# Nine instead of seven up-projection pairs in seven products each, placed two and two, in a one-core encoder layer

## The chip, the core and the metric

The kernel runs on one core of one Trainium2 chip. The metric is the time of one execution in microseconds (us), as the device reports it; three runs of the kernel before are shown, and one further execution was profiled. A lower time is better.

## What is computed

One layer of an encoder with 512 tokens and a model width of 1024, all in float32. Three sub-layers follow one another, each between two RMS norms and added to the residual: token mixing (an attention group and a gated recurrent group, "HGRN"), cross-attention into 256 memory tokens, and a gated MLP. The change is mostly about the MLP:

```python
def conv_ffn(h, w_up, conv_w, conv_b, w_down):
    u = h @ w_up                       # 512 x 1024 times 1024 x 5632
    up = jnp.pad(u, ((0, 0), (half, half), (0, 0)))
    acc = conv_b
    for j in range(CONV_W):
        acc = acc + up[:, j:j + n] * conv_w[j]
    gate, val = jnp.split(acc, 2, axis=-1)
    return (jax.nn.silu(gate) * val) @ w_down
```

The 5632 columns of `w_up` are 22 blocks of 128 gate columns and 22 blocks of 128 value columns. Gate block i and value block i are called pair i here.

## The kernel before, in words

**Products in three parts.** Every float32 operand of a large product is split into a high part and a low part, and `mm3` (lines 277 to 280) issues three matmuls for each product: high by high (L278), high by low (L279), low by high (L280). In the up-projection the weights are the stationary operand, so L280 is the one that loads the low part of the weights.

**Units.** Weights are read in units of 128 x 1024 elements (512 KB). `load_w` loads a unit into a `raw` buffer by a DMA of SyncE (SP). There are four such buffers in the up-projection, two called `raw` and two called `tmp`. `issue` then makes the high part `wh` on ScalarE (ACT, L222) and the low part `wl`: on VectorE (DVE) as `raw - wh` (L224), or by writing `-wh` into `wl` (ACT, L229) and letting a DMA of GpSimd's (POOL) queue add the weights from DRAM onto it (L230). `wh` and `wl` have four buffers each, so unit n can only be written when TensorE (PE) has finished unit n-4. The order in which units are consumed is the list `plan`.

**Pairs in seven products.** An ordinary pair takes two units, each of 8 x 3 matmuls of 512 columns. The pairs named in `UP_S` use Strassen's scheme with seven half-size products instead of eight (`strassen_pair`): 7 x 4 x 3 matmuls of 256 columns. Such a pair takes four units, consumed in this order: *diag* (two blocks of weights, products w11 and w22), *side* (product t2 in its first half, w21 in its second), *sums* (t3, t1) and *last* (t4). Only diag and side are loaded. The rest are sums of blocks that `add_blocks` makes on VectorE: `both` from the diag and the side block (L197), then t2 in place over the first half of the side's raw buffer (L200), then the last (L204). So the side's high part cannot be made before L200. Products are followed by small additions (L1144 to L1155) and by a convolution on ScalarE and VectorE (L1069 to L1083).

Which part of `wl` comes by the GpSimd DMA is said by `LOW_FROM`: all of a diag unit, the second half (columns 512 on, the block w21) of a side unit.

**Additions ahead.** The down-projection later uses the same scheme with larger blocks; its weight sums are made in DRAM by 24 accumulating DMAs of GpSimd's queue (L251). They are issued behind certain units, each after a one-column copy (`mark`, L236) that waits for the unit's low part. `adds_at` says behind which units: those in `ADDS_AT` and, in the up-projection, one or two at each ordinary pair.

**The HGRN head.** In `hgrn_core` the keys and queries of a head are copied into a pair order (L632) before the first level of a recurrence; all these copies run on ScalarE, except the one of the queries of head 1, which runs on VectorE. Its first-level product is L647 on TensorE with both copies as operands; each level then scales keys and queries in place (L673), copies the keys (L644) and forms the next product (L647). TensorE's order there is interleaved with the projection of head 2.

Functions and line numbers follow.

Of the kernel before, what the change touches and what calls it, by code (L numbers as in the profile page):

```python
# [20 lines left out]
T = 512  # L21
# [4 lines left out]
FF = 2816  # L26
NF = FF // P
EPS = 1e-6
UP_S = (6, 8, 10, 12, 14, 16, 18)
N_MIX, N_WHOLE = 66, 110 - 2 * len(UP_S)  # L30
N_DOWN = N_WHOLE + 4 * len(UP_S)
N_UNITS = N_DOWN + 42
# [5 lines left out]
UP_PRODUCTS = (("w11", 0), ("w22", 1), ("t2", 0), ("w21", 1), ("t3", 1), ("t1", 0), ("t4", 0))  # L38
LAY_AHEAD, LOAD_AHEAD = 3, (7, 5)
SIDES_AT = (19, 20)  # L40
LOW_FROM = {"diag": 0, "side": 512}
SEEDS_AT = frozenset(range(28, 46)) | frozenset(range(60, 66))
ADDS_AT = frozenset(range(56, 62))
NEG_GROUP = frozenset((p, 1) for p in (2, 5, 6))
AHEAD = 3
HOLD_BLOCK = 4
# [1 line left out]
NEG_SCALAR = frozenset(range(9, 33))  # L48
NEG_POOL = frozenset(range(33, 42))
# [9 lines left out]
def pat(t, off, dims):  # L59
    a = t[:]  # L60
    return bass.AP(tensor=a.tensor, offset=a.offset + off, ap=[list(a.ap[0])] + [list(d) for d in dims])
# [28 lines left out]
def layer(tc, io, out):  # L90
    nc = tc.nc
# [53 lines left out]
    plan = [("w", i) for i in range(N_MIX)]  # L145
    whole, adds_at = N_MIX, set(ADDS_AT)
    for i in range(NF):
        if i in UP_S:
            plan += [(kind, UP_S.index(i)) for kind in ("diag", "side", "sums", "last")]
        else:  # L150
            if i >= 2:
                adds_at.update((len(plan), len(plan) + (i - 1 not in UP_S)))
            plan += [("w", whole), ("w", whole + 1)]
            whole += 2
    assert len(plan) == N_DOWN and whole == N_WHOLE
# [52 lines left out]
    def issue():  # L208
        i = issued[0]
        issued[0] += 1  # L210
        raw = raws.popleft() if raws else load_w()
        kind = plan[i][0] if i < N_DOWN else "w"
        if kind == "diag" and not raws:
            raws.append(load_w())
        if raw is None:
            raw = pair_sums[kind]
        wh = wp.tile([P, 1024], F32R, name="wh", tag="wh")
        wl = wp.tile([P, 1024], F32R, name="wl", tag="wl")
        if raw.shape[1] < 1024:
            wh, wl = wh[:, :raw.shape[1]], wl[:, :raw.shape[1]]  # L220
        by_dma = 0 if i in NEG_SCALAR or i in NEG_POOL else LOW_FROM.get(kind, raw.shape[1])
        nc.scalar.copy(wh, raw)  # L222
        if by_dma:
            last_low[0] = nc.vector.tensor_sub(wl[:, :by_dma], raw[:, :by_dma], wh[:, :by_dma].bitcast(F32)).ins  # L224
        if by_dma < raw.shape[1]:
            if i in NEG_POOL:
                nc.gpsimd.tensor_scalar(wl, wh.bitcast(F32), -1.0, 0.0, op0=ALU.mult, op1=ALU.add)
            else:
                nc.scalar.mul(wl[:, by_dma:], wh[:, by_dma:].bitcast(F32), -1.0)  # L229
            nc.gpsimd.dma_start(wl[:, by_dma:], source(i)[:, by_dma:], accum_op=ALU.add)  # L230
        add_blocks(kind, raw, raws[0] if raws else None)
        pending.append((wh, wl))
        if i in SEEDS_AT:
            seeds.popleft()()
        if i in adds_at and adds:
            with tc.issue_after(nc.gpsimd.tensor_copy(mark, wl[:, 0:1].bitcast(F32)).ins):  # L236
                adds.popleft()()
# [216 lines left out]
    raw = rawp.tile([P, 1024], F32, name="raw", tag="raw")  # L454
# [163 lines left out]
    def hgrn_core(h):  # L618
        while h not in heads:
            yield None  # L620
        q, qk, tt = heads[h]
# [4 lines left out]
        diag = a[:, :, 0, :]  # L626
# [2 lines left out]
        nc.vector.scalar_tensor_tensor(out=ksum, in0=qk[:, 1, 1, :], scalar=oml[:, 1, h:h + 1], in1=ksum,  # L629
                                       op0=ALU.mult, op1=ALU.add)  # L630
        for side, to in ((1, kc), (0, qc)):
            (nc.vector.tensor_copy if (h, side) == (1, 0) else nc.scalar.copy)(  # L632
                to, pat(qk, side * 2 * T, [[2, T // 2], [T + 1, 2]]))
        o = bank("c").rearrange("p (b n) -> p b n", b=NB)
        for b in range(NB):
            nc.tensor.matmul(o[:, b, :], ksum[:, blk(b)], q[:, blk(b)], start=True, stop=True)
# [710 lines left out]
```

## Time and profile before

| | |
|---|---|
| median of three runs | 816.1 us (815.86 to 816.65) |
| the profiled execution | 816.71 us |
| its span in the trace | 813.8 us |
| TensorE busy | 803.3 us (99% of the span), 4426 matmuls |
| weight loads on TensorE busy | 691.0 us (85%) |
| VectorE busy | 574.7 us (71%) |
| ScalarE busy | 482.1 us (59%) |
| GpSimd busy | 136.9 us (17%) |
| mean granted TensorE clock | 0.998 of full speed |

The profiled execution is longer than its span by 2.9 us, which lies before the first and after the last instruction of the trace. It is 0.6 us longer than the median of the three runs. Matmuls overlap in the trace, so a matmul's pace is the distance between two starts and not the duration of one row. The up-projection lies at about 500 to 700 us of the span, the down-projection behind it.

### The profile page before, as it was taken

How to read it: one execution, taken by the hardware profiler on the slowest of the kernel's cores; microseconds unless marked ns; L12 is line 12 of the kernel's file. 1: busy time of each engine (PE TensorE's matmuls, PEld its weight loads, DVE VectorE, ACT ScalarE, POOL GpSimd, SP SyncE). 2: the span in 40 equal slices, each digit the busy share in tenths (PEclk: the TensorE clock that was granted, in tenths of full speed). 3: DMA queues.
4: the chain of work that ended last, by engine and by line, in shares of the span. 5: the costliest groups of instructions: out<-in, count | busy, mean ns of one | idle time of the engine just before them, and what ended most of it. 6: DMA issues, size and time to landing. Idle time of an engine off the chain costs nothing.

```text
span 813.8 us, 11771 instructions
## 1 busy us (share of the span) xinstructions
PE 803.3 (99%) x4426; PEld 691.0 (85%) x4426; DVE 574.7 (71%) x868; ACT 482.1 (59%) x796; POOL 136.9 (17%) x213
## 2 busy tenths in 40 slices
PE   9999999999999999999999999999999999999996
PEld 7888888889998887888888898899999998888885
DVE  5456587469886865855453767987777788888765
ACT  5675757459988874644543553665555545566651
POOL 0111201053233102301010311211111111000301
PEclk9999999999999999999999999999999999999999
DMA  8685645569899753256634158776665677278852
GB/s 296 202 259 139 160 103 117 118 159 247 229 250 254 182 172 126 78 181 157 180 117 142 33 164 208 154 200 166 179 171 143 150 200 178 91 208 278 239 130 104
DMA packets 42457, 139.61 MB, mean 172 GB/s; under 512 B 5280, under 2 KB 6560, under 8 KB 42400
## 3 DMA queue, kind: packets, MB, share of 16 engines
q1 hardware_dynamic: 28944, 97.43, 35.5%
q0 software_dynamic: 12160, 38.54, 26.2%
q10 hardware_dynamic: 1296, 2.89, 1.0%
q8 instruction: 34, 0.56, 0.3%
q14 instruction: 23, 0.19, 0.1%
HBM read 135.17 MB, written 25.17 MB: 197 GB/s over the span
## 4 chain that ended last, share of the span: by engine, by line
PE 92%; DVE 3%; ACT 2%; issue 1%; POOL 1%; DMA 0%; DVEq 0%; POOLq 0%; SPq 0%; ACTq 0%
PE ps_b L279 10%; PE ps_b L280 10%; PE ps_b L278 10%; PE ps_s L278 6%; PE ps_s L280 6%; PE ps_s L279 6%; PE ps_o L278 5%; PE ps_o L279 5%; PE ps_o L280 5%; PE ps_c L278 5%; PE ps_c L280 5%; PE ps_c L279 5%; PE ps_c L647 3%; PE ps_o L893 2%; PE ps_s L872 2%; PE ps_o L882 2%
## 5 line engine op out<-in xcount | busy, mean ns | idle before, releaser
L222 ACT CAST wh<-raw 128x1024 fp32r<-128x1024 f32 x110 | 113.7, 1035 | 114.6 <-PE ps_b L279 35.3
L224 DVE TENSOR_TENSOR wl<-raw,wh 128x1024 fp32r<-128x1024 f32 (+1 forms) x77 | 92.3, 1201 | 72.2 <-ACT wh L222 72.0
L278 PE MATMUL ps_b<-big,wh 128*128 128x512 f32 (+1 forms) x344 | 122.3, 355 | 0.0
L280 PE MATMUL ps_b<-big,wl 128*128 128x512 f32 (+1 forms) x344 | 121.2, 352 | 0.0
L279 PE MATMUL ps_b<-big,wh 128*128 128x512 f32 (+1 forms) x344 | 121.2, 352 | 0.0
L280 PEld LDWEIGHTS ps_b<-big,wl 128*128 128x128 f32 x344 | 65.1, 189 | 8.5 <-DMA wl<-in_wu_dram 0.2
L278 PEld LDWEIGHTS ps_b<-big,wh 128*128 128x128 f32 x344 | 65.1, 189 | 8.3
L279 PEld LDWEIGHTS ps_b<-big,wh 128*128 128x128 f32 x344 | 65.1, 189 | 8.1
L673 DVE TENSOR_TENSOR big<-big 128x512 f32<-128x512 f32 x64 | 47.2, 755 | 9.6 <-PE ps_c L647 4.0
L278 PE MATMUL ps_s<-wh,big 128*128 128x512 f32 (+1 forms) x140 | 53.4, 383 | 0.0
L279 PE MATMUL ps_s<-wl,big 128*128 128x512 f32 (+1 forms) x140 | 53.3, 381 | 0.0
L280 PE MATMUL ps_s<-wh,big 128*128 128x512 f32 (+1 forms) x140 | 53.0, 379 | 0.0
L230 POOL DMA_DIRECT2D wl<-in_w_dram x33 | 29.3, 887 | 126.7 <-ACT wl L229 91.5
L122 DVE TENSOR_TENSOR big<-ps_o,big 128x512 fp32r<-128x512 f32 x54 | 36.9, 687 | 15.0 <-ACT big L121 13.4
L121 ACT CAST big<-ps_o 128x512 fp32r<-128x512 f32 x54 | 31.7, 588 | 18.5 <-PE ps_o L996 7.5
L278 PE MATMUL ps_s<-big,wh 128*128 128x256 f32 (+1 forms) x120 | 40.0, 334 | 0.0
L279 PE MATMUL ps_s<-big,wh 128*128 128x256 f32 (+1 forms) x120 | 40.0, 333 | 0.0
L280 PE MATMUL ps_s<-big,wl 128*128 128x256 f32 (+1 forms) x120 | 40.0, 333 | 0.0
L278 PE MATMUL ps_o<-wh,big 128*128 128x512 f32 (+1 forms) x102 | 39.2, 385 | 0.0
L279 PE MATMUL ps_c<-big,wh 128*128 128x256 f32 (+1 forms) x120 | 39.1, 326 | 0.0
L278 PE MATMUL ps_c<-big,wh 128*128 128x256 f32 (+1 forms) x120 | 39.1, 326 | 0.0
L280 PE MATMUL ps_c<-big,wl 128*128 128x256 f32 (+1 forms) x120 | 39.1, 326 | 0.0
(315 smaller groups left out, 2149.3 us busy)
## 6 DMA issues: line engine op xcount, KB each, us to landing
raw<-in_w_dram SPq DMA_DIRECT2D x91, 512.0 KB, 3.6
wl<-in_w_dram POOLq DMA_DIRECT2D x33, 512.0 KB, 7.3
sum_t<-in_wd_dram SPq DMA_DIRECT2D x20, 512.0 KB, 6.3
tmp<-in_wu_dram SPq DMA_DIRECT2D x14, 512.0 KB, 6.9
sum_t<-in_wd_dram POOLq DMA_DIRECT2D x10, 512.0 KB, 8.4
sum_t<-sum_t POOLq DMA_DIRECT2D x10, 512.0 KB, 7.5
big<-sum_t SPq DMA_DIRECT2D x10, 512.0 KB, 4.7
raw<-sum_t SPq DMA_DIRECT2D x10, 512.0 KB, 4.4
```

The source lines that it names most:

```text
L121: nc.scalar.copy(hi, src)
L122: (eng or nc.vector).tensor_sub(lo, src, hi.bitcast(F32))
L222: nc.scalar.copy(wh, raw)
L224: last_low[0] = nc.vector.tensor_sub(wl[:, :by_dma], raw[:, :by_dma], wh[:, :by_dma].bitcast(F32)).ins
L230: nc.gpsimd.dma_start(wl[:, by_dma:], source(i)[:, by_dma:], accum_op=ALU.add)
L278: nc.tensor.matmul(o, a[0], b[0], start=start, stop=False, skip_group_check=again)
L279: nc.tensor.matmul(o, a[0], b[1], start=False, stop=False, skip_group_check=again)
L280: last_mm[0] = nc.tensor.matmul(o, a[1], b[0], start=False, stop=stop, skip_group_check=again).ins
L647: nc.tensor.matmul(o[:, b, :], kc[:, blk(b)], qc[:, blk(b)] if m == 1 else pat(qk, b * P, [[2 * m, P // (2 * m)], [T + m, 2], [1, m]]), st ...
L673: nc.vector.tensor_tensor(out=c, in0=c, in1=pat(tt, toff + off, [[2, npair], [gap, 2], [0, m]]), op=ALU.mult)
L872: nc.tensor.matmul(s, qT[h // 4][:, h % 4, blk(qb)], kT[:, 2 * (h // 4) + c, :], start=c == 0, stop=c == 1)
L882: nc.tensor.transpose(o[:, c, :], e[:, 0, blk(c)], ident)
```

## The change

```diff
-UP_S = (6, 8, 10, 12, 14, 16, 18)
+UP_S = (6, 8, 9, 11, 12, 14, 15, 17, 18)
...
-LOW_FROM = {"diag": 0, "side": 512}
+LOW_FROM = {"diag": 0, "next": 1024, "side": 512}
...
-ADDS_AT = frozenset(range(56, 62))
+ADDS_AT = frozenset(range(56, 63))
...
             if i >= 2:
-                adds_at.update((len(plan), len(plan) + (i - 1 not in UP_S)))
+                adds_at.update((len(plan), len(plan) + (i + 1 not in UP_S)))
...
-        by_dma = 0 if i in NEG_SCALAR or i in NEG_POOL else LOW_FROM.get(kind, raw.shape[1])
+        close = kind == "diag" and UP_S[plan[i][1]] - 1 in UP_S
+        by_dma = 0 if i in NEG_SCALAR or i in NEG_POOL else LOW_FROM.get("next" if close else kind, raw.shape[1])
...
         for side, to in ((1, kc), (0, qc)):
-            (nc.vector.tensor_copy if (h, side) == (1, 0) else nc.scalar.copy)(
-                to, pat(qk, side * 2 * T, [[2, T // 2], [T + 1, 2]]))
+            nc.scalar.copy(to, pat(qk, side * 2 * T, [[2, T // 2], [T + 1, 2]]))
```

It does five things. Nine pairs instead of seven are done in seven products. Four of them (9, 12, 15, 18) now follow directly on another such pair (8, 11, 14, 17), with no ordinary pair between; pair 6 still stands alone. The low part of the diag unit of these four "second" pairs is made by VectorE alone, while their side unit keeps the GpSimd DMA for its second half. The additions ahead of the down-projection are put behind other units: one more in the stage before, one instead of two at pair 5 and none of the ones that stood at pairs that are no longer ordinary; there are 24 as before. The query copy of HGRN head 1 goes from VectorE to ScalarE. In the changed file the lines from 222 to 632 stand one further down (L224 is L225, L230 is L231, L632 is L633); lines from 635 on are the same.

VectorE's order around the units of a pair in seven products before the change: here pair 16, which stands behind the ordinary pair 15 (`tmp_5891` is its diag, `tmp_5932` its side in raw form, `tmp_5925` to `tmp_5927` belong to the products of pair 14):

```order
L224 TENSOR_TENSOR wl<-raw,wh 128x1024
L1146 TENSOR_TENSOR tmp_5925<-ps_s,tmp_5925 128x256
L224 TENSOR_TENSOR wl<-raw,wh 128x1024
L1148 TENSOR_TENSOR tmp_5926<-ps_c,tmp_5925 128x256
L197 TENSOR_TENSOR both<-tmp_5891,tmp_5932 128x1024
L1150 TENSOR_TENSOR tmp_5926<-ps_s,tmp_5925 128x256
L200 TENSOR_TENSOR tmp_5932<-both,tmp_5891 128x512
L1151 TENSOR_TENSOR tmp_5927<-ps_c,tmp_5926 128x512
L1155 TENSOR_TENSOR ps_b<-ps_b,tmp_5926 128x256
L204 TENSOR_TENSOR tmp_6061<-tmp_5932 128x512
L224 TENSOR_TENSOR wl<-tmp_5932,wh 128x512
```

In the changed kernel, the same place for pair 15, the second of two (here diag and side lie in `raw`, and `tmp_5981` to `tmp_5983` belong to the products of pair 14):

```order
L225 TENSOR_TENSOR wl<-raw,wh 128x1024
L197 TENSOR_TENSOR both<-raw 128x1024
L1146 TENSOR_TENSOR tmp_5981<-ps_c,tmp_5981 128x256
L200 TENSOR_TENSOR raw<-both,raw 128x512
L204 TENSOR_TENSOR tmp_6053<-raw 128x512
L1148 TENSOR_TENSOR tmp_5982<-ps_o,tmp_5981 128x256
L225 TENSOR_TENSOR wl<-raw,wh 128x512
L1150 TENSOR_TENSOR tmp_5982<-ps_c,tmp_5981 128x256
L1151 TENSOR_TENSOR tmp_5983<-ps_o,tmp_5982 128x512
L225 TENSOR_TENSOR wl<-both,wh 128x1024
L1155 TENSOR_TENSOR ps_s<-ps_s,tmp_5982 128x256
```

The whole diag's low part (first row) now stands ahead of the sums L197 and L200, and the side's preparation follows within the products of the pair in front instead of behind an ordinary pair.

GpSimd's queue around pair 6, before:

```order
L251 DMA sum_t_0_2734<-sum_t_0_1734 128x1024
L230 DMA wl<-in_wu_dram 128x1024
L236 COPY mark<-wl 128x1
L251 DMA sum_t_1_2795<-sum_t_1_1872 128x1024
L230 DMA wl<-in_wu_dram 128x512
```

and in the changed kernel, there and on to pairs 8 and 9:

```order
L252 DMA sum_t_1_2795<-sum_t_1_1872 128x1024
L231 DMA wl<-in_wu_dram 128x1024
L231 DMA wl<-in_wu_dram 128x512
L237 COPY mark<-wl 128x1
L252 DMA sum_t_2_2916<-sum_t_2_1917 128x1024
L231 DMA wl<-in_wu_dram 128x1024
L231 DMA wl<-in_wu_dram 128x512 x2
```

No addition stands between the diag's and the side's DMA of pair 6 any more, and at pairs 8 and 9 there are one DMA for a diag and two for sides.

TensorE's order at the first levels of HGRN head 1, before (`tmp_894` is the query copy, `tmp_893` the key copy, L278 to L280 the projection of head 2):

```order
L278 MATMUL ps_b<-big,wh 128x512
L647 MATMUL ps_c<-tmp_894,tmp_893 128x128 x4
L279 MATMUL ps_b<-big,wh 128x512
L647 MATMUL ps_c<-big,tmp_914 128x128 x4
L280 MATMUL ps_b<-big,wl 128x512
```

and in the changed kernel:

```order
L279 MATMUL ps_b<-big,wh 128x512
L280 MATMUL ps_b<-big,wh 128x512
L647 MATMUL ps_c<-tmp_894,tmp_893 128x128 x4
L281 MATMUL ps_b<-big,wl 128x512
L647 MATMUL ps_c<-big,tmp_914 128x128 x4
```

Each of the two first-level products stands one projection matmul later.

## Rows read from the trace of the kernel before

**Rows 1.** The page: busy time by engine, and the chain that ended last by engine

```profile
PE 803.3 (99%) x4426; PEld 691.0 (85%) x4426; DVE 574.7 (71%) x868; ACT 482.1 (59%) x796; POOL 136.9 (17%) x213
...
PE 92%; DVE 3%; ACT 2%; issue 1%; POOL 1%; DMA 0%; DVEq 0%; POOLq 0%; SPq 0%; ACTq 0%
```

**Rows 2.** Stretches: length, busy (count) of PE, PEld, DVE, ACT, POOL; clock, DMA, GB/s

```profile
100.00:120.00 20.00, 19.28 (x121) 16.05 (x120) 18.98 (x35) 10.24 (x16) 1.73 (x2) 1.00 0.46 103
564.14:575.04 10.90, 10.90 (x50) 9.02 (x49) 8.58 (x13) 6.68 (x10) 2.84 (x4) 1.00 1.02 261
575.04:585.12 10.08, 10.08 (x86) 10.07 (x85) 7.59 (x11) 5.03 (x7) 1.05 (x2) 1.00 0.37 100
```

**Rows 3.** Timeline of PE in pair 6 (start, duration, instruction): start of product w21

```profile
537.23 0.28 PE L279 MATMUL ps_b<-big,wh 128*128 128x256 f32 x1
537.54 0.39 PE L280 MATMUL ps_b<-big,wl 128*128 128x256 f32 x1
537.76 0.28 PE L278 MATMUL ps_b<-big,wh 128*128 128x256 f32 x1
```

**Rows 4.** Timeline of PEld: the weight load of that L280, and its wait

```profile
537.53 0.19 PEld L280 LDWEIGHTS ps_b<-big,wl 128*128 128x128 f32 x1 [0.23 <-DMA wl<-in_wu_dram]
```

**Rows 5.** Timeline of POOL: an addition ahead, then the side DMA of pair 6

```profile
524.81 0.84 POOL L251 DMA_DIRECT2D sum_t<-sum_t  x1 [0.30 <-issue]
529.99 0.88 POOL L230 DMA_DIRECT2D wl<-in_wu_dram  x1 [4.33 <-ACT wl L229]
```

**Rows 6.** Timeline of POOL: diag and side DMA of pair 12

```profile
586.25 0.88 POOL L230 DMA_DIRECT2D wl<-in_wu_dram  x1 [4.45 <-ACT wl L229]
589.79 0.86 POOL L230 DMA_DIRECT2D wl<-in_wu_dram  x1 [2.66 <-ACT wl L229]
```

**Rows 7.** DMA issues, KB, us to landing: seven sides; those at 586.25, 589.79; 522.82; 601.91

```profile
wl<-in_wu_dram POOLq DMA_DIRECT2D x7, 256.0 KB, 7.5
...
wl<-in_wu_dram POOLq DMA_DIRECT2D x1, 512.0 KB, 8.5
...
wl<-in_wu_dram POOLq DMA_DIRECT2D x1, 256.0 KB, 6.7
...
wl<-in_wu_dram POOLq DMA_DIRECT2D x1, 512.0 KB, 5.5
...
sum_t<-sum_t POOLq DMA_DIRECT2D x1, 256.0 KB, 5.2
```

**Rows 8.** Timeline of ACT: a cast behind PE (pair 10); cast and negation of pair 6's side

```profile
578.00 1.05 ACT L222 CAST wh<-raw 128x1024 fp32r<-128x1024 f32 x1 [0.95 <-PE ps_b L279]
...
527.94 1.04 ACT L222 CAST wh<-tmp 128x1024 fp32r<-128x1024 f32 x1
529.06 0.63 ACT L229 ACTIVATE wl<-wh 128x512 fp32r<-128x512 f32 x1
```

**Rows 9.** Timeline of DVE in pair 10: a low part, and the sums for pair 12

```profile
579.08 1.22 DVE L224 TENSOR_TENSOR wl<-raw,wh 128x1024 fp32r<-128x1024 f32 x1 [0.46 <-ACT wh L222]
...
583.43 1.22 DVE L197 TENSOR_TENSOR both<-tmp,tmp 128x1024 f32<-128x1024 f32 x1
584.56 0.42 DVE L1150 TENSOR_TENSOR tmp<-ps_o,tmp 128x256 f32<-128x256 f32 x1
584.90 0.69 DVE L200 TENSOR_TENSOR tmp<-both,tmp 128x512 f32<-128x512 f32 x1
```

**Rows 10.** Timelines of ACT, DVE and PE at the first two levels of HGRN head 1

```profile
100.16 0.85 ACT L632 COPY tmp<-big 128x512 f32<-128x512 f32 x1
...
100.61 0.50 DVE L632 COPY tmp<-big 128x512 f32<-128x512 f32 x1
101.04 2.15 DVE L673 TENSOR_TENSOR big<-big 128x512 f32<-128x512 f32 x2
...
102.14 0.47 PE L279 MATMUL ps_b<-big,wh 128*128 128x512 f32 x1
103.33 1.20 PE L647 MATMUL ps_c<-big,tmp 128*128 128x128 f32 x8 [0.72 <-DVE big L673]
```

## The prediction

> **What bounds the kernel now.** I read the page's busy times and its chain first. TensorE is busy for 99% of the span, and it holds 92% of the chain that ended last [rows 1]. So time is won by giving TensorE less to do, and lost wherever it has to wait. Then I read the up-projection by stretches. From 564.14 to 575.04 us lies an ordinary pair, from 575.04 to 585.12 a pair in seven products: 10.90 and 10.08 us, both filled by TensorE without a gap, at the full granted clock of 1.00 [rows 2]. The 48 matmuls of 512 columns have a pace of 10.90/48 = 0.227 us, the 84 of 256 columns one of 10.08/84 = 0.120. In the second kind the weight loads are busy for 10.07 of 10.08 us, which is why halving the columns does not quite halve the pace.
>
> The waits come next. In the whole up-projection TensorE waits once: in pair 6 the first low-part matmul of w21 starts 0.31 us after the one ahead of it and the next 0.22 later, where 0.12 is the pace, so 0.29 us are lost [rows 3]. Its weight load waited for a DMA into `wl` [rows 4]. That is the side's GpSimd DMA, issued at 529.99 [rows 5]; with the 7.5 us that such a DMA takes in the median [rows 7] it landed at 537.5. Last, in the token mixing, TensorE waits for VectorE at one place, the second level of HGRN head 1 [rows 10], in a stretch where VectorE is busy for 18.98 of 20 us [rows 2].
>
> **Term 1: two pairs fewer in whole products.** Two pairs go from 10.90 to 10.08 us: 2 x 0.82 = 1.64 us gained, if TensorE stays fed.
>
> The Trainium skill's page "TensorE: Matmul & The Clock Gate", section "Back-to-back issue gap", gives N/2.4 ns plus 2.5 between warm matmuls of N columns. An estimate from that page has pairs of 48 x 215.8 = 10.36 and 84 x 109.2 = 9.17 us and a gain of 2.4 us for both, some 0.7 more than the sum here; the trace disagrees, with 0.227 and 0.120 us, and the measured pace stays.
>
> **Term 2: the addition ahead at pair 5.** The order shows that the addition issued at 524.81, between the diag and the side DMA of pair 6 [rows 5], is issued before both now. The side DMA no longer queues behind 512 KB, and 0.3 us earlier is enough to end the wait of rows 3: 0.29 us gained (ends 0 and 0.29). The addition that moves into the stage before has the 24 marks' usual kind of place, behind a low part made long before, and nothing waits for it there. The additions that move to pairs 19 to 21 serve the down-projection's sixth product, far later. Both count nothing.
>
> **Term 3: the query copy.** On VectorE it took 0.50 us, in front of the two L673 that TensorE then waits for [rows 10]. But the first L673 also needs ScalarE's key copy, from 100.16 to 101.01, and started at 101.04, right behind it. So VectorE's chain wins next to nothing there. ScalarE's second copy, of about the same 0.85 us, ends near 101.8; the first-level product waits for it, about 0.5 us later than now. In the new order one more projection matmul stands ahead of each of the two products. At 103.3, where the second-level product can start as before, TensorE has therefore one matmul more behind it: 0.23 us gained. I take 0.25, with ends of 0.7 (the wait of 0.72 gone altogether) and a loss of 0.4 (0.5 us late, not made up).
>
> **Term 4: a new wait, in the second pair of each two.** Here lies the risk. `wh` and `wl` of unit n come free when TensorE ends unit n-4. Behind an ordinary pair that leaves the side more than 13 us; behind another seven-product pair it leaves its own 24+12+24 matmuls, 7.2 us. I follow the second pair's side, from the moment (0) at which TensorE starts the first pair's side. The second diag's cast starts 0.08 later (pair 10's side starts at 575.04 + 24 x 0.12 = 577.92, the cast at 578.00 [rows 8]). VectorE's low part starts 1.08 behind the cast (579.08 [rows 9]): at 1.16. L197, L1146 and L200 follow as in the changed order. The large ones start 1.13 after one another (583.43 to 584.56), the small one takes 0.34 (to 584.90) [rows 9]: 2.30, 3.43, 3.77. L200 ends at 4.46. The side's cast can start at 4.55, its negation 1.12 behind that (527.94 to 529.06 [rows 8]) at 5.67, ending at 6.30. GpSimd issues 0.30 later (529.69 to 529.99 [rows 5, 8]): at 6.60.
>
> TensorE reaches the second side after 84 matmuls, at 10.08, and w21's first low-part matmul 14 later, at 11.76; its weight load falls 0.12 earlier, at 11.64. So the DMA has 5.0 us. Each longer landing is a wait, four times over (pairs 9, 12, 15, 18).
>
> What does it take? The seven sides before took 7.5 us in the median [rows 7], but they queue behind their own diag DMA: pair 12's diag landed at 586.25 + 8.5 = 594.75 and its side at 589.79 + 6.7 = 596.49, only 1.74 behind [rows 6, 7]. The second pair's diag has no DMA now. A 512 KB one with little beside it took 5.5 [rows 7]; half the bytes should be some 1.7 shorter, 3.8. The other 256 KB accumulation without a diag ahead, at 601.91, took 5.2 [rows 7]. In the changed kernel two SyncE loads, into the second pair's own raw buffers, start some 2 us before it and just with it, as one or two do at 601.91. So I take 5.1, nearest to that row: 0.1 us of wait, 0.3 to 0.4 with its after-effects for all four. The ends are 3.8 (no wait) and 7.5 (2.5 each, 10 in all).
>
> The Trainium skill's page "DMA: Bandwidth & Descriptors", section "Anatomy of one DMA — SWDGE (gpsimd) path", gives 2.0 us plus the bytes at 436 GB/s. By an estimate from that page 256 KB land after 2.6 us and TensorE never waits, 0.3 less than the sum; no row here is as short, the lowest of this size being 5.2.
>
> VectorE's extra low parts, 4 x 1.22 us, replace DMAs and lie beside TensorE's work: VectorE has 4.8 us free in each 21 [rows 2]. What they delay is counted above, since they stand ahead of L197. The units sums and last are ready some 3 us or more before their use. A first pair's diag DMA has as much time from its free buffer as before, and it had 1.5 us to spare (594.75 against 596.26); the loads and the addition now reach closer to it, which I cost at nothing, with up to 0.5 us for each of three as the other end.
>
> **Sum.** -1.64 - 0.29 - 0.25 + 0.3 = -1.9 us. The profiled execution took 816.71, so it would take 814.8; the median of the runs shown lies 0.6 below it, at 816.1, and the forecast for a median is 814.2.
>
> **Rivals.** What a measurement of this kernel can tell from no change is about 0.2%, 1.63 us: faster means below 814.5, slower above 817.7.
>
> - *The second sides land as the seven sides do.* The place is the weight load of w21 in pairs 9, 12, 15, 18. It needs a landing of 5.6 us to eat the gains of 2.18 (0.55 each) and of 6.0 to be slower by 0.2%. With 6.7 to 7.5 the waits are 4 x 1.7 to 2.5 = 6.7 to 10 us and the time is 820.6 to 824. For it: no side yet landed below 6.7, and pair 6 shows the wait itself. Against it: all of them stood behind a DMA of twice their size. Chance 0.15.
> - *The same wait, middling.* Landings of 5.3 to 5.9, from the two loads beside the DMA, or the first diags losing their spare: 1.1 to 3.6 us in all, 815.0 to 817.5. This is no change to be measured. Chance 0.25, and 0.05 for the copies in series on ScalarE costing 0.4 instead of giving 0.25, at 814.9.
> - *No wait at all,* and a mixing stage that wins more: 813.3 to 813.9. The page's rule on DMA times would have it so. Chance 0.12. That TensorE's own gain is the 2.4 of the other page, at 813.5, has 0.01; the stretches of rows 2 exclude it nearly.
> - That the change does not do what it says is out: the order shows 84 matmuls of 256 columns for each of nine pairs and no GpSimd DMA at the four diags.
>
> **How the numbers follow.** The forecast, waits of 0.15 or less each, has 0.42, at 814.2. Faster by over 0.2% are the forecast and the third rival, 0.55; within 0.2% the second, 0.30; slower the first, 0.15. The range reaches from 813.2 (no wait, most of the copy's gain) to 817.5 (the middling wait in full). It leaves out the first rival and a little below, some 0.17.
>
> **What would show it.** Right: pairs in seven products still take 10.08 us each; the wait in pair 6 is gone; HGRN head 1's second level starts with less idle time on TensorE; the four second sides are issued about 6.6 us after the first side's start and land about 5 us later. Wrong: a weight load of L280 that waits for `wl<-in_wu_dram` by over 0.5 us at w21 of a second pair, by which the first or the second rival holds; a wait for VectorE's low parts in these pairs, which I count as hidden; or a wait in the token mixing longer than the 0.72 us of before.

## The result and the profile after

The changed kernel takes **818.36 us** (median of 7 runs, 817.31 to 820.71) against 816.1 for the kernel before (7 runs beside it); the ratio is 1.0029 with a 95% interval of 1.0017 to 1.0041. It is slower by about 2.3 us, where 1.9 less was forecast, and it lies above the range of 813.2 to 817.5. A second series of runs, below, gave 817.83 with a ratio of 1.0022 (1.0012 to 1.0031).

The profiled execution took 820.71 us, the longest of the seven. Its page, busy time by engine, answers to [rows 1]:

```profile
span 818.9 us, 11944 instructions
...
PE 805.7 (98%) x4498; PEld 694.9 (85%) x4498; DVE 588.2 (72%) x889; ACT 485.8 (59%) x803; POOL 139.5 (17%) x213
```

Three stretches of the changed kernel answer to [rows 2]: the ordinary pair 13, then pair 14 and pair 15 in seven products. Columns: stretch, length, busy time (count) of PE, PEld, DVE, ACT, POOL; clock, DMA share, GB/s.

```profile
610.56:621.47 10.91, 10.91 (x51) 9.01 (x49) 8.50 (x13) 7.08 (x11) 1.72 (x2) 1.00 0.81 204
621.47:631.54 10.07, 10.07 (x86) 10.07 (x84) 8.74 (x13) 5.32 (x7) 0.66 (x1) 1.00 0.17 53
631.54:642.20 10.66, 10.33 (x87) 10.13 (x85) 10.16 (x16) 5.87 (x8) 1.48 (x3) 1.00 0.58 139
```

The pace is what it was: 10.91 for an ordinary pair and 10.07 for one in seven products. Pair 15, the second of its two, takes 0.59 more. Its TensorE is idle at one place, and the same place stands in pairs 9, 12 and 18. The timeline of PE shows it in pairs 9 and 12 (start, duration, instruction, idle time before it and what ended that):

```profile
569.51 0.28 PE L280 MATMUL ps_b<-big,wh 128*128 128x256 f32 x1
570.38 0.39 PE L281 MATMUL ps_b<-big,wl 128*128 128x256 f32 x1 [0.59 <-DMA wl<-in_wu_dram]
...
601.42 0.28 PE L280 MATMUL ps_b<-big,wh 128*128 128x256 f32 x1
603.46 0.39 PE L281 MATMUL ps_b<-big,wl 128*128 128x256 f32 x1 [1.76 <-DMA wl<-in_wu_dram]
```

This is the first low-part matmul of w21, and what ends its idle time is the side's GpSimd DMA. Start to start, where the pace is 0.12, 0.75 us are lost in pair 9, 1.92 in pair 12, and by the same reading 0.49 in pair 15 and 0.56 in pair 18. Behind the longest wait TensorE runs at the lower of its clock levels for 3.3 us, as the stretches from that wait on show:

```profile
601.42:603.46 2.04, 0.28 (x4) 0.08 (x2) 2.04 (x3) 0.63 (x1) 0.00 (x0) 1.00 0.08 16
603.90:607.20 3.30, 3.30 (x18) 3.30 (x17) 1.28 (x3) 1.04 (x1) 1.22 (x2) 0.50 0.81 178
607.30:612.00 4.70, 4.70 (x36) 4.44 (x35) 4.25 (x8) 2.24 (x3) 0.00 (x0) 1.00 0.86 214
```

A granted clock of 0.50 is 1.2 GHz. In that stretch the matmuls start every 0.21 us instead of 0.12, which lost 1.4 us more.

Where the time went is best read from the distances between the starts of the same matmuls in the PE timelines, in us:

| stage | before | changed, profiled | changed, again | all by VectorE |
|---|---|---|---|---|
| span's start to first projection | 27.52 | 28.13 | 28.27 | 27.80 |
| to behind the HGRN heads' start (130 us) | 101.64 | 101.73 | 101.66 | 101.66 |
| to the up-projection | 360.09 | 360.16 | 360.21 | 360.19 |
| to pair 6 | 43.55 | 43.55 | 43.54 | 43.55 |
| **pair 6 to the down-projection** | **168.91** | **173.02** | **170.80** | **166.98** |
| to the last matmul | 104.89 | 105.10 | 105.05 | 105.08 |
| from there to the end of the span | 7.20 | 7.21 | 7.27 | 6.94 |
| outside the span | 2.91 | 1.81 | 1.76 | 1.78 |
| the execution | 816.71 | 820.71 | 818.56 | 813.98 |

The last two columns are of experiments below. The first row varied between 27.1 and 28.5 in the twelve further profiles, whatever the kernel, so it is chance. The one row that carries the result is pair 6 to the down-projection.

### The profile page after: what moved, and what is told of

It is laid out like the page before. It is cut to its first block, busy times and chain, and to the rows that moved or that the text cites. A ratio compares the mean times of both kernels' runs of the same rounds, so it can differ in the third digit from the quotient of the medians.

```text
span 818.9 us, 11944 instructions
## 1 busy us (share of the span) xinstructions
PE 805.7 (98%) x4498; PEld 694.9 (85%) x4498; DVE 588.2 (72%) x889; ACT 485.8 (59%) x803; POOL 139.5 (17%) x213
## 5 line engine op out<-in xcount | busy, mean ns | idle before, releaser
L225 DVE TENSOR_TENSOR wl<-raw,wh 128x1024 fp32r<-128x1024 f32 (+1 forms) x75 | 87.7, 1171 | 68.5 <-ACT wh L223 67.6
L281 PE MATMUL ps_b<-big,wl 128*128 128x512 f32 (+1 forms) x364 | 128.4, 353 | 3.1 <-DMA wl<-in_wu_dram 3.1
L279 PE MATMUL ps_b<-big,wh 128*128 128x512 f32 (+1 forms) x364 | 129.0, 354 | 0.0
L280 PE MATMUL ps_b<-big,wh 128*128 128x512 f32 (+1 forms) x364 | 127.6, 351 | 0.0
L281 PEld LDWEIGHTS ps_b<-big,wl 128*128 128x128 f32 x364 | 69.1, 190 | 12.9 <-DMA wl<-in_wu_dram 4.1
L280 PEld LDWEIGHTS ps_b<-big,wh 128*128 128x128 f32 x364 | 69.1, 190 | 8.6
L279 PEld LDWEIGHTS ps_b<-big,wh 128*128 128x128 f32 x364 | 69.1, 190 | 8.4
L280 PE MATMUL ps_s<-wl,big 128*128 128x512 f32 (+1 forms) x140 | 53.3, 380 | 0.0
L231 POOL DMA_DIRECT2D wl<-in_w_dram x33 | 29.3, 889 | 124.8 <-ACT wl L230 89.6
L122 DVE TENSOR_TENSOR big<-ps_o,big 128x512 fp32r<-128x512 f32 x54 | 36.9, 687 | 15.1 <-ACT big L121 13.4
L279 PE MATMUL ps_s<-big,wh 128*128 128x256 f32 (+1 forms) x128 | 38.9, 304 | 0.0
L280 PE MATMUL ps_s<-big,wh 128*128 128x256 f32 (+1 forms) x128 | 38.8, 303 | 0.0
L279 PE MATMUL ps_o<-big,wh 128*128 128x512 f32 (+1 forms) x112 | 38.6, 345 | 0.0
L280 PE MATMUL ps_o<-big,wh 128*128 128x512 f32 (+1 forms) x112 | 38.5, 344 | 0.0
L281 PE MATMUL ps_o<-big,wl 128*128 128x512 f32 (+1 forms) x112 | 38.5, 344 | 0.0
```

The costliest lines, as they stand in the source:

```text
L122: (eng or nc.vector).tensor_sub(lo, src, hi.bitcast(F32))
L279: nc.tensor.matmul(o, a[0], b[0], start=start, stop=False, skip_group_check=again)
L280: nc.tensor.matmul(o, a[0], b[1], start=False, stop=False, skip_group_check=again)
L281: last_mm[0] = nc.tensor.matmul(o, a[1], b[0], start=False, stop=stop, skip_group_check=again).ins
```

## The experiments

My theory after the result: the whole pairs pay what was forecast, and the DMAs of the second sides land too late, by the traffic beside them. Twelve kernels were run, each against the kernel before on the same chip.

### 1. The second sides by VectorE

```diff
-        close = kind == "diag" and UP_S[plan[i][1]] - 1 in UP_S
+        close = kind in ("diag", "side") and UP_S[plan[i][1]] - 1 in UP_S
```

> The changed kernel, with the low part of the side units of pairs 9, 12, 15 and 18 made wholly by VectorE too, so that no DMA stands in front of w21 there. Theory (the landing of these four DMAs is what costs, 5.7 to 7.1 us against the 5.0 that the pair leaves; the seven-product pairs themselves pay as predicted): the four waits of 0.5 to 1.9 us go, nothing takes their place, and the time is 814.2 to 814.8 against 816.1 before. VectorE's four low parts grow from 0.69 to 1.22 us, 2.1 in all, beside TensorE's work. Rival 1 (VectorE or ScalarE is short in two such pairs in a row): waits for VectorE's low parts or ScalarE's casts appear in the same pairs, and the time stays at 816 or above. Rival 2 (pairs in a row run at a slower pace): no waits, but 84 matmuls take more than 10.08 us and the time stays above 815.5.

Measured: 815.19 us against 815.98, ratio 0.9991 (0.9982 to 1.0000). The four waits are gone, and some 3 us with them. But 0.4 to 1.0 of the expected gain is missing, and the timeline of PE shows a wait that no theory had, at the first diag of pair 11, an ordinary pair's successor (pair 14 has another of 0.30):

```profile
585.86 0.28 PE L280 MATMUL ps_s<-big,wh 128*128 128x256 f32 x1
586.64 0.38 PE L281 MATMUL ps_s<-big,wl 128*128 128x256 f32 x1 [0.50 <-DMA wl<-in_wu_dram]
```

The DMA that it waited for, issued at 576.68 behind an addition at 572.18 (timeline of POOL), and its landing (DMA issues of that moment, KB, us to landing):

```profile
572.18 0.84 POOL L252 DMA_DIRECT2D sum_t<-sum_t  x1
576.68 0.88 POOL L231 DMA_DIRECT2D wl<-in_wu_dram  x1 [3.67 <-ACT wl L230]
```

```profile
wl<-in_wu_dram POOLq DMA_DIRECT2D x1, 512.0 KB, 9.9
```

So a first diag's DMA has no spare left once TensorE does not wait elsewhere.

### 2. The query copy alone

```diff
-            (nc.vector.tensor_copy if (h, side) == (1, 0) else nc.scalar.copy)(
-                to, pat(qk, side * 2 * T, [[2, T // 2], [T + 1, 2]]))
+            nc.scalar.copy(to, pat(qk, side * 2 * T, [[2, T // 2], [T + 1, 2]]))
```

> The kernel before, with only the query copy of HGRN head 1 on ScalarE. Term 3 of the prediction: 0.25 us less, 815.85. Theory now (in the changed trace TensorE's first-level product starts 0.47 us late, waiting for ScalarE's second copy, and its second level 0.41 late instead of 0.96, so the stretch gains 0.03): 816.1, no difference within 0.2 us. Rival (the two copies in series cost more in other executions): 816.4 or more.

Measured: 816.31 against 815.98, ratio 1.0006 (0.9997 to 1.0014): no gain. The stage up to 130 us took 101.68 us, 101.64 before. The changed kernel's timeline of PE shows why, and answers to [rows 10]:

```profile
102.53 1.16 PE L647 MATMUL ps_c<-tmp,tmp 128*128 128x128 f32 x8 [0.30 <-ACT tmp L633]
103.44 0.47 PE L281 MATMUL ps_b<-big,wl 128*128 128x512 f32 x1
104.08 0.36 PE L647 MATMUL ps_c<-big,tmp 128*128 128x128 f32 x1 [0.16 <-DVE big L678]
```

The second level waits less than the 0.72 us of before, but the first level now waits for ScalarE's second copy. Both together lose 0.88 us start to start, where 0.96 were lost; in the length of the stage even that 0.08 is not seen.

### 3. The additions alone

```diff
-ADDS_AT = frozenset(range(56, 62))
+ADDS_AT = frozenset(range(56, 63))
...
-                adds_at.update((len(plan), len(plan) + (i - 1 not in UP_S)))
+                adds_at.update((len(plan), len(plan) + (i + 1 not in UP_S)))
```

> The kernel before, with only the places of the additions changed: one instead of two at pair 5, one more in the stage before, and the rule that looks at the pair behind instead of the pair ahead. Term 2 of the prediction: the wait of 0.29 us in pair 6 goes, 815.8. Rival (the changed trace still waits 0.20 there, because its side was issued 2 us later, behind a weight load that landed 1.2 us later at the end of the cross-attention): the addition ahead only moves the traffic, the wait stays and the time is 816.1.

Measured: 816.14 against 815.98, ratio 1.0003 (0.9994 to 1.0011). In its trace pair 6 does not wait, and pair 6 to the down-projection takes 168.62 us, 0.29 less, as forecast. But experiment 2, whose additions stand as before, shows no wait there either and the same 168.62, and the changed kernel, whose additions stand as here, lost 0.30 there in its first profile and nothing in its second (experiment 10). So this wait comes and goes between executions; what the move is worth stays open, between 0 and 0.29 us.

### 4. The second diags by DMA

```diff
-LOW_FROM = {"diag": 0, "next": 1024, "side": 512}
+LOW_FROM = {"diag": 0, "next": 0, "side": 512}
```

> The changed kernel, with the low part of the diag units of pairs 9, 12, 15 and 18 by GpSimd's DMA, as for the other pairs. By the chain of the prediction the diag's DMA is issued some 2.5 us after its buffer comes free and used 7.2 us after it, so that it has 4.7 us to land, where 512 KB took 5.5 to 8.5 before: a wait of 1 to 4 us at w11 of these pairs; the side behind it lands later too, up to 2 us more of wait at w21. Theory: 4 times 1 to 5 us more than the changed kernel without its own four waits, 820 to 832. Rival (DMA landing is no bound, the waits come from something else in the pair): about 818.4 as the changed kernel.

Measured: 818.37 against 815.98, ratio 1.0030 (1.0019 to 1.0040), the same as the changed kernel. The number is the rival's, the cause is the theory's, at and below its low end. GpSimd's timeline for pair 9, and PE's at w11 of pairs 9 and 18:

```profile
559.46 0.86 POOL L231 DMA_DIRECT2D wl<-in_wu_dram  x1 [11.48 <-ACT wl L230]
561.91 0.85 POOL L231 DMA_DIRECT2D wl<-in_wu_dram  x1 [1.59 <-DVE wl L225]
```

```profile
565.14 0.38 PE L281 MATMUL ps_b<-big,wl 128*128 128x256 f32 x1 [0.59 <-DMA wl<-in_wu_dram]
...
661.51 0.38 PE L281 MATMUL ps_b<-big,wl 128*128 128x256 f32 x1 [1.39 <-DMA wl<-in_wu_dram]
```

TensorE waits for the diag now, 0.76, 1.08, 0.30 and 1.55 us start to start, and for no side: without the diag's low part in VectorE's queue the side is issued 5.0 us behind the start of the first pair's side (556.94 to 561.91) instead of 6.5. So the part of the change that moves the diag to VectorE wins nothing here: it takes away the wait at w11 and makes the one at w21.

### 5. The side's second half first

```diff
+        early = kind == "side" and UP_S[plan[i][1]] - 1 in UP_S
+        if early:
+            nc.scalar.copy(wh[:, 512:], raw[:, 512:])
+            nc.scalar.mul(wl[:, 512:], wh[:, 512:].bitcast(F32), -1.0)
+            nc.gpsimd.dma_start(wl[:, 512:], source(i)[:, 512:], accum_op=ALU.add)
+            nc.scalar.copy(wh[:, :512], raw[:, :512])
+        else:
+            nc.scalar.copy(wh, raw)
...
-        if by_dma < raw.shape[1]:
+        if by_dma < raw.shape[1] and not early:
```

> The changed kernel, with the side unit of pairs 9, 12, 15 and 18 prepared in two halves: the second half (block w21) is cast, negated and handed to GpSimd's DMA first, since it does not need the sums of VectorE (L200), and the first half is cast behind it. The DMA stays, with its 256 KB; only its issue moves, from some 6.5 us behind the start of the first pair's side to some 4.3 (buffer free at 2.9, cast and negation of 512 columns 0.6 each, 0.3 to the issue). Theory (the chain ahead of the issue and a landing of 5.7 to 7.1 us together miss the need at 11.64 by 0.5 to 1.9): landed at 10.0 to 11.4, the four waits go, and the time is 814.8 to 815.6, near that of the kernel whose second sides are VectorE's (815.19). Rival (earlier issue only meets other traffic, the landing is set by when the two loads beside it end): landing 8 us or more, the waits stay, 817.5 or more.

Measured: 814.52 against 816.28, ratio 0.9976 (0.9966 to 0.9985). No wait of TensorE for a DMA that costs more than 0.15 us is left in the up-projection. The DMA of pair 9 was issued 4.5 us behind the start of the first pair's side (556.73 to 561.26). Landings of the four, pairs 9 and 12 shown (5.1 and 5.3 in the others):

```profile
wl<-in_wu_dram POOLq DMA_DIRECT2D x1, 256.0 KB, 5.0
...
wl<-in_wu_dram POOLq DMA_DIRECT2D x1, 256.0 KB, 7.2
```

So with 2 us more to land, the same DMA costs next to nothing. At pair 12 that is just enough: it landed at 599.70, where the matmul that needs it was due at 599.69, and 0.15 us were lost there.

### 6. Experiment 1 with four additions elsewhere

```diff
-ADDS_AT = frozenset(range(56, 63))
+ADDS_AT = frozenset(range(52, 63))
...
-            if i >= 2:
+            if i >= 2 and not (i - 1 in UP_S and i + 1 in UP_S):
```

> The kernel with VectorE's second sides (815.19), without the additions at the ordinary pairs 7, 10, 13 and 16 that stand between two pairs in seven products; the four additions are made in the cross-attention instead, behind units 52 to 55. In that kernel TensorE still waits for the diag DMA of the first pairs 11 and 14 (0.66 and 0.30 us, with after-effects 1.1 in all), which is issued 4.5 us behind such an addition of 512 KB and took 9.5 to 9.9 us to land. Theory (the addition stands in that DMA's way): landing about 8 us, no wait in the up-projection, 814.1 to 814.5. Rival 1 (the weight loads and the gain loads make it late, not the addition): the waits stay, 815.2. Rival 2 (the additions now slow the loads of the cross-attention): new waits there, above 815.5.

Measured: 820.20 against 816.28, ratio 1.0038 (1.0025 to 1.0051). The theory and the second rival are both right. Pair 6 to the down-projection took 166.98 us, without a wait, and the DMAs of the first diags of pairs 11 and 14 landed after 8.5 and 7.3 us instead of 9.9 and 9.5. But the stage before the up-projection took 365.5 us instead of 360.2. The timeline of PE there, two stretches of it, and the DMA issues between 352 and 368 us:

```profile
365.85 0.39 PE L281 MATMUL ps_b<-big,wl 128*128 128x512 f32 x1
369.73 0.60 PE L279 MATMUL ps_b<-big,wh 128*128 128x512 f32 x1 [3.49 <-DVE big L964]
```

```profile
366.00:369.70 3.70, 0.24 (x2) 0.00 (x0) 1.82 (x2) 1.54 (x2) 0.18 (x1) 1.00 0.96 238
369.70:372.30 2.60, 2.57 (x7) 1.99 (x8) 0.60 (x1) 1.54 (x2) 0.82 (x1) 0.55 0.80 241
```

```profile
raw<-in_w_dram SPq DMA_DIRECT2D x4, 512.0 KB, 6.3
sum_t<-in_wd_dram POOLq DMA_DIRECT2D x3, 512.0 KB, 9.2
```

These four weight loads are of two kinds. The first two, of which one ended ahead of the additions and one reached into them, took 3.2 and 3.3 us; the two that started among the three additions (at 357.42 and 360.44) took 9.3 and 10.0. In experiment 7, without additions there, the median is 3.2. ScalarE's cast waited for one of them for 7.62 us, VectorE behind it, and TensorE behind VectorE. After this wait, too, the granted clock fell to 0.50, from 370.0 to 373.3 us; the 0.55 of the second stretch is a mean over both levels.

### 7. All low parts by VectorE

```diff
-LOW_FROM = {"diag": 0, "next": 1024, "side": 512}
+LOW_FROM = {}
...
-        by_dma = 0 if i in NEG_SCALAR or i in NEG_POOL else LOW_FROM.get("next" if close else kind, raw.shape[1])
+        by_dma = 0 if i in NEG_SCALAR or i in NEG_POOL else LOW_FROM.get(kind, raw.shape[1])
```

> The changed kernel with all low parts of all nine pairs made by VectorE, no accumulating DMA in the up-projection's pairs at all. Against the kernel with VectorE's second sides (815.19) that adds 1.22 us for each first diag and 0.53 for each first side, in cycles of 32 us in which VectorE is busy for 28.1 to 28.8: 30 of 32. Theory (only the landing of DMAs makes TensorE wait in these pairs): all waits go, 814.0 to 814.5. Rival (VectorE at 94% is the next bound: its low parts or the sums L197 and L200 come late): waits of TensorE for VectorE or ScalarE in the second pairs, 815.5 or more.

Measured: **814.20** against 816.28, ratio 0.9974 (0.9963 to 0.9985): faster than both kernels, and the best of the study. The waits of PE in the whole kernel that are longer than 0.15 us (engine, tile and line, waited for: us in all, times, longest) all lie before 250 us of the span, none in the MLP, and in a stretch of the up-projection TensorE is full beside a VectorE that is busy for 30.49 of 32 us:

```profile
PE ps_b L467 <- DVE tmp L448: 1.3, 1, 1.3
PE ps_c L647 <- ACT tmp L644: 0.5, 1, 0.5
PE ps_b L279 <- DVE big L122: 0.4, 1, 0.4
PE ps_c L647 <- ACT tmp L633: 0.3, 1, 0.3
PE ps_c L647 <- DVE big L678: 0.2, 1, 0.2
```

```profile
607.00:639.00 32.00, 32.00 (x222) 29.94 (x221) 30.49 (x43) 16.05 (x21) 1.32 (x2) 1.00 0.41 126
```

The up-projection from pair 6 takes 166.98 us, 1.93 less than before: the 1.64 of the two pairs and the 0.29 of pair 6's wait.

### 8. One more pair, placed apart

```diff
-UP_S = (6, 8, 10, 12, 14, 16, 18)
+UP_S = (6, 8, 10, 12, 14, 16, 18, 20)
...
-ADDS_AT = frozenset(range(56, 62))
+ADDS_AT = frozenset(range(56, 65))
```

> The kernel before, with one more pair in seven products, 20, behind the ordinary pair 19, so that no two such pairs meet; its three additions go to the cross-attention. This is term 1 by itself, at half size: an ordinary pair of 10.90 us becomes one of 10.08, 0.82 less, 815.2. Rival 1 (a further pair pays less or nothing, whatever its neighbours): 815.9. Rival 2 (the down-projection's first operands or its loads, which follow pairs 20 and 21, come late): waits behind 690 us, 816 or more.

Measured: 816.20 against 816.28, ratio 0.9998 (0.9989 to 1.0007). Rival 2 holds. From pair 6 to the down-projection it takes 167.92 us, 0.99 less, of which 0.29 is the wait in pair 6 that did not come here; from there to the last matmul 105.67, 0.78 more. The start of the down-projection, before and here:

```profile
700.00:720.00 20.00, 20.00 (x90) 16.57 (x89) 19.27 (x21) 13.49 (x18) 0.00 (x0) 1.00 0.48 153
```

```profile
700.00:720.00 20.00, 19.85 (x86) 15.67 (x85) 20.00 (x23) 12.40 (x16) 0.00 (x0) 1.00 0.46 158
```

VectorE was busy for 19.27 of these 20 us before, and is for all of them here, so TensorE loses time behind it. This run also shows a side's DMA with no load of SyncE's beside it: pair 20's, issued at 672.87, landed in 3.6 us. Yet its own diag's DMA of 512 KB, issued at 670.03 and landed after 5.0 us, lay ahead of it on the same queue:

```profile
wl<-in_wu_dram POOLq DMA_DIRECT2D x1, 512.0 KB, 5.0
wl<-in_wu_dram POOLq DMA_DIRECT2D x1, 256.0 KB, 3.6
```

So in this one row a side behind its diag's DMA, as all seven sides were before, is not slow.

### 9. The two loads held back

```diff
-    raws = deque()
+    raws, near_raw = deque(), [None]
...
+        if close:
+            near_raw[0] = raw
+        if kind == "side" and UP_S[plan[i][1]] - 1 in UP_S:
+            for t in (wl.bitcast(F32)[:, 1023:], raw[:, :1], near_raw[0][:, :1]):
+                nc.gpsimd.tensor_copy(mark, t)
```

> The changed kernel, with the two weight loads that the second side's preparation releases (into the second pair's own raw buffers; they started 2.0 us before the side's DMA and just with it) held back until that DMA has landed: three one-column copies on GpSimd behind the DMA, the first reading the landed low part, the others the two raw buffers. Issue, size and need of the side's DMA stay. Theory (what made it 5.7 to 7.1 us instead of the 5.0 that it has is the traffic of these two loads beside it; with nothing beside it 256 KB took 3.6 and 4.0 in other runs of this case): landing 3.6 to 4.5 us, the four waits go, and the time is near that of the kernel with early halves (814.5), 814.4 to 815.6. Rival (a lone accumulating DMA of 256 KB takes 5 us or more behind VectorE's and ScalarE's work, whatever the loads do): landing 5.2 or more, waits of 0.2 to 2 stay, 816.5 or more. Rival 2 (the held loads come late for the next pair): waits for ScalarE's casts at pairs 11, 14, 17.

Measured: 814.82 against 815.95, ratio 0.9985 (0.9976 to 0.9995). This is the decisive one. In the changed kernel SyncE's loads into the second pair's raw buffers start at 562.39 and 564.21 (SP's row holds both), the second just ahead of the side's DMA at 564.41. The timelines of SP and POOL there, and the issues at that DMA:

```profile
562.39 2.15 SPq L189 DMA_DIRECT2D raw<-in_wu_dram  x2
...
564.41 0.86 POOL L231 DMA_DIRECT2D wl<-in_wu_dram  x1 [15.50 <-DVE wl L225]
```

```profile
raw<-in_wu_dram SPq DMA_DIRECT2D x1, 512.0 KB, 4.8
wl<-in_wu_dram POOLq DMA_DIRECT2D x1, 256.0 KB, 5.9
```

In this kernel the DMA is issued at the same place (6.5 us behind the start of the first pair's side), and the loads come behind its landing:

```profile
563.56 0.85 POOL L231 DMA_DIRECT2D wl<-in_wu_dram  x1 [15.52 <-DVE wl L225]
567.26 0.19 POOL L236 COPY mark<-wl 128x1 f32<-128x1 f32 x1 [2.85 <-DMA wl<-in_wu_dram]
...
567.72 1.07 SPq L189 DMA_DIRECT2D raw<-in_wu_dram  x2
```

```profile
wl<-in_wu_dram POOLq DMA_DIRECT2D x1, 256.0 KB, 3.6
```

The four land in 3.6, 3.8, 3.7 and 3.6 us instead of 5.9, 7.1, 5.7 and 5.7, and TensorE waits for none. Neither rival holds.

### 10. The changed kernel again

> The changed kernel once more, on this chip. Its profiled execution was the slowest of seven (820.71 against a median of 818.36) and had one wait of 1.9 us with 3.3 us at half the granted clock behind it. Theory (landing of the second sides, 5.7 us and more, by chance longer): 817.5 to 819.0, four waits of 0.4 to 1.0 us in the up-projection, which is 170 to 171 us long from pair 6 to the down-projection against 167.0 without waits. Rival (the long wait and the low clock are of every execution, at pair 12): the same wait of 1.9 us at the same place.

Measured: 817.83 against 815.95, ratio 1.0022 (1.0012 to 1.0031). Its profiled execution, 818.56, has the same four waits:

```profile
PE ps_b L281 <- DMA wl<-in_wu_dram: 2.8, 4, 1.4
```

Start to start they lose 0.35, 1.51, 0.82 and 0.76 us, with landings of 5.5, 6.7, 6.0 and 5.9. The longest is at pair 12 again, so that part of the rival holds; behind it the granted clock stayed at 1.00, so the low clock is not of every execution.

### 11. Ten pairs, all by VectorE

```diff
-UP_S = (6, 8, 9, 11, 12, 14, 15, 17, 18)
+UP_S = (5, 6, 8, 9, 11, 12, 14, 15, 17, 18)
...
-ADDS_AT = frozenset(range(56, 63))
+ADDS_AT = frozenset(range(56, 65))
```

> The kernel with all low parts of the pairs in seven products on VectorE (814.20), with pair 5 in seven products too, so ten in all and 5 and 6 side by side. If a pair still pays 0.82 us where no DMA is needed: 813.4. Rival (VectorE is at 95% there already and still has the sums of the left operand and norms to do near pair 5, or additions moved into the cross-attention cost there): waits for VectorE around 520 to 540 us, 814.2 or more.

This is an edit of experiment 7. Measured: 817.80 against 815.95, ratio 1.0021 (1.0012 to 1.0030): the rival. The timeline of PE, and the stretch around it:

```profile
525.20 0.38 PE L279 MATMUL ps_b<-big,wh 128*128 128x256 f32 x1 [0.93 <-ACT big L121]
526.70 0.38 PE L280 MATMUL ps_b<-big,wh 128*128 128x256 f32 x1 [1.12 <-DVE big L122]
```

```profile
515.00:535.00 20.00, 17.64 (x100) 15.71 (x99) 20.00 (x25) 9.09 (x12) 0.00 (x0) 0.91 0.16 54
```

VectorE is busy for all 20 us, since the sums of the left operand (L1114, L122) are still being made there, and TensorE waits for them at pair 5. Start to start these two waits lose 1.1 and 1.4 us, and behind them the granted clock was 0.50 from 527.4 to 530.7, which is why the stretch's mean is 0.91.

### 12. Experiment 7 with the copy back on VectorE

> The kernel with all low parts of the pairs in seven products on VectorE (814.20), with the query copy of HGRN head 1 back on VectorE as before. Theory (the copy's place gives and costs nothing: the stretch around it took 101.64 us before and 101.65 to 101.73 with it moved): 814.2 within 0.3 us. Prediction's term 3: 0.25 us slower, 814.45.

Its edit is experiment 2's, turned round. Measured: 814.41 against 815.95, ratio 0.9980 (0.9971 to 0.9989), beside 0.9974 for experiment 7: no difference that these runs can tell. Its profile has two waits in the MLP that experiment 7's has not, both for VectorE: TensorE loses 0.34 us in pair 6 and 0.71 at the start of the down-projection, start to start. The copy has no part there. So with VectorE this full, short waits for it come in some executions.

## Why the prediction was wrong

**Term 1 was right.** Two pairs at 0.82 us each were won in full: 166.98 us from pair 6 to the down-projection, without waits, against 168.91 with pair 6's wait of 0.29. The 2.4 us that I estimated by a formula of the Trainium skill's page "TensorE: Matmul & The Clock Gate", section "Back-to-back issue gap", are not borne out. That section of the Trainium skill gives the formula for an isolated matmul and says that in a stream of weight loads and matmuls both set the spacing, so I applied it where it does not belong. The trace agrees with the section in this: in pair 14 the weight loads are busy for 10.07 of 10.07 us. What I did not count is 0.2 us more in the down-projection (105.05 to 105.10, before 104.89), where VectorE is nearly full, as experiment 8 shows; that VectorE is the cause of these 0.2 is not shown.

**Term 2** is open between 0 and its 0.29; the wait of rows 3 was one that some executions have.

**Term 3 was wrong, by its own step.** I let the first-level product come later and the second level start when it did before. It started later as well: the first product waited for ScalarE's second copy (0.30), and what the later place in TensorE's order won was lost there. Gain 0.25 forecast; in the traces 0.08 at these two waits and none in the stage up to 130 us (101.65 to 101.73 in the ten profiles with the copy moved, 101.64 to 101.70 in the four without), and nothing in the times.

**Term 4 failed, and it decides.** Its chain came out right: issue 6.60 us after the start of the first pair's side, and 6.54 measured (557.87 to 564.41); the low-part matmul due at 11.76, and due at 569.63, 11.76 behind 557.87. What released the DMA last was VectorE's low part of the side's first half, which the chain had not named; it ended 0.06 us behind the negation, so little came of that. The step that failed is "So I take 5.1, nearest to that row", the landing. The eight landings of the two profiles lie between 5.5 and 7.1 us, in the middle at 5.9. The row at 601.91, 5.2 us [rows 7], had two loads near it as well, but the first 0.6 us ahead of it and the other some 2 us behind. Here the second load starts with the DMA, and experiment 9 shows that these two loads are the whole difference: without them 3.6 to 3.8. So my lower end, 3.8, was the price without traffic, and the price with it was beyond the one I took. That is 0.3 us forecast, and 3.8 (170.80 less 166.98) to 5.5 measured (173.02 less 166.98 is 6.0, of which 0.5 was lost in pair 6; 1.4 of the 5.5 come from the lower clock).

When the loads start matters too. In experiment 5 one starts with the DMA and the other 1.6 us behind, much as at 601.91, and three of its four landings are 5.0, 5.1 and 5.3: the price that I took, for loads that come later than those of the changed kernel do. That my lower end of 3.8 came out was luck. The row that I halved for it, at 522.82, had not little beside it: an addition until 524.75, another from 524.81 and a load from 524.26. A diag's DMA without loads took 5.0 (experiment 8).

The missing thought is where the loads come from. The chain that I followed to the side's DMA also frees the two raw buffers that SyncE waits for: L200 is the last to read the diag's (it ends at 562.32 for pair 9, and a load starts at 562.39), and VectorE's low part, right behind the side's cast, the last to read the side's (timeline of DVE in the changed kernel):

```profile
561.64 0.68 DVE L200 TENSOR_TENSOR raw<-both,raw 128x512 f32<-128x512 f32 x1
...
563.49 0.69 DVE L225 TENSOR_TENSOR wl<-raw,wh 128x512 fp32r<-128x512 f32 x1
```

So the loads are released by the same work that releases the DMA, in each of the four pairs, and meet it by construction, not by chance.

Of the rivals, the first and the second named the right place and the right cause. The waits of 0.35 to 1.92 us lie between their prices: 5.3 to 5.9 us of landing was the second's, 6.7 to 7.5 the first's. The time of 818.36 falls between their ranges. The two together had 0.40, and the forecast 0.42 on the strength of one row. What I held against the first rival, that the seven sides stood behind a DMA of twice their size, does not stand up: pair 20's side in experiment 8 did so too and landed in 3.6 us. What the seven had, and it had not, is two weight loads in flight beside each. The Trainium skill's page "DMA: Bandwidth & Descriptors", section "Anatomy of one DMA — SWDGE (gpsimd) path", by which I estimated 2.6 us, gives no price for a transfer that shares the queues' engines with two loads; the runs show 3.6 us at best.

**What I costed at nothing** was partly not nothing: the first diags' DMA. Their spare of 1.5 us was gone in experiment 1 (0.66 and 0.30 us of wait at pairs 11 and 14), because the addition stands 4.5 us ahead of them; in experiment 6, without these additions, the wait is gone. In the changed kernel the waits of the second sides hid this. And the diag's low part on VectorE, one of the five edits, wins nothing by itself (experiment 4): it stands ahead of L197 and L200 and delays the side's issue by 1.6 us (4.97 us behind the start of the first pair's side, 6.54 with it).

## What to carry to other kernels

When a transfer has little time to land, list what the same chain of work releases for the other queues, and price the transfer with that traffic beside it: here 3.6 us became 5.5 to 7.1. Of a row taken as the nearest, look at what lay beside it and when. And where a change shifts work between an engine and a queue, try the plain form first: with every low part on VectorE the same nine pairs gain 2 us, though VectorE is then busy for 95% of the stretch.

## What the runs showed of the hardware

- An accumulating DMA of 256 KB on GpSimd's queue landed in 3.6 to 3.8 us with no load beside it (experiments 8 and 9), and in 5.0 to 7.2 with two loads of 512 KB started around it: in 5.0 to 5.3 where these start with it and 1.6 us behind (experiment 5), in 5.5 to 6.0 where they start 2.0 us ahead and just before it (both profiles of the changed kernel), pair 12 aside. At pair 12 it was slowest in these three profiles (7.1, 6.7, 7.2), and with the loads held back it took 3.8 there too. One thing sets these three landings apart from the other nine: a packet on the queue that the profile calls `instruction` lies in each of them and in none of the nine (DMA of the changed kernel from 596.33 to 603.41 us: packets, MB, share of 16 engines). But in experiments 4 and 9 one lies in pair 12's landing as well, and there pair 12 took 6.6 and 3.8 us, hardly more than the other pairs. So that it is the cause is not shown.

```profile
q8 instruction: 1, 0.02, 1.2%
```

- The granted clock fell to 0.50, 1.2 GHz, for 3.3 us each, behind a wait of TensorE of 1.92 us (the first profile of the changed kernel), behind one of 3.65 us (experiment 6), and behind two of 1.1 and 1.4 us in a row (experiment 11). It stayed at 1.00 behind single waits of 1.51 (experiment 10) and 1.55 (experiment 4).
- The time outside the span was 2.9 us in the profile before, 2.6 in experiment 3 and about 1.8 in all others, so spans of single executions are not compared here; the distances between matmuls are.
